# Windowed attention in units of 64 queries of two heads, with 320 keys, in place of 128 queries of one head with 384

## The chip, the cores and the metric

The kernel runs on one core of a Trainium2 chip. The core has five engines with a queue each: TensorE (PE), whose weight loads are shown apart as PEld, VectorE (DVE), ScalarE (ACT), GpSimd (POOL), and SyncE (SP), which issues the transfers. The metric is the time of one execution on the device in microseconds; of the kernel before three runs are known, with 440.9 us as their median.

## The reference, cut to what matters

One encoder layer over 1024 tokens of 1024 numbers: a projection into queries, keys, values and gates of two groups of heads, two kinds of attention, gates, an output projection, and a layer norm. The change is in group B, the windowed attention with shared keys. It has 8 query heads and 2 key heads of 64 numbers; a query sees the keys at most 128 tokens away, and a learned sink logit joins the softmax of each head.

```python
def windowed_gqa_with_sink(q, k, v, sink):          # q: (1, 1024, 8, 64); k, v: (1, 1024, 2, 64)
    ...                                             # blocks of 128 queries, bands of 384 keys
    s = jnp.einsum('bnqkgd,bnjkd->bnkgqj', qb, k_band).astype(jnp.float32) * (D ** -0.5)
    valid = (jnp.abs(k_off - q_off) <= SWA_WINDOW)[None] & (k_abs >= 0) & (k_abs < S)
    s = jnp.where(valid[None, :, None, None], s, MASK_VALUE)
    p = jax.nn.softmax(jnp.concatenate([s, sink_col], axis=-1), axis=-1)[..., :-1]
    out = jnp.einsum('bnkgqj,bnjkd->bnqkgd', p.astype(v.dtype), v_band)
...
    y_b = windowed_gqa_with_sink(qb, kb, v_b, sink)
    mixed = jnp.concatenate([y_a * jax.nn.silu(z_a), y_b * jax.nn.silu(z_b)], axis=-1)
    y = jnp.einsum('bse,ed->bsd', mixed, w_out[layer])
    x = layer_norm(DEEPNORM_ALPHA * x + y, ln_gain[layer], ln_bias[layer])
```

## The kernel before, in words

**The work.** The projection of x is made of 128x512 matmuls in f16 (L430), with weights and x split into a high and a low f16 part, so that three passes give one f32 product. What it delivers is turned to queries and keys, which are split into high and low parts again (high by ACT at L298 or L300, low by DVE at L304 or by POOL at L306), and group B's get their rotary positions on the way (L364 to L368). The weights of a projection are scaled and split on the way in as well: ACT makes the high part (L240), POOL scales and makes the low part (L245, L246).

**Units.** Attention runs in 128 units, first 64 of group B and then 64 of group A. A unit (g, p, j, t) of group B is the block t of 128 queries of head j of head pair p; the order is p, then j, then t. Four units in a row are a quad. What is done for a unit i and for its quad q, by stage:

- `stage_qk`: two matmuls (L860, L861: the query tile holds high and low parts on its 128 partitions, and is multiplied by the keys' high and then low parts) put scores for up to three blocks of 128 keys, 384 columns, in a bank of PSUM; a unit at either end of the sequence has two blocks, 256 columns. DVE adds the mask `bm`, changes the sign, writes the scores to `sn` in SBUF and keeps the row's minimum, the sink included, as `nm` (L870, called "the reduction" below; the profile shows its accumulator read as a row of its own).
- `stage_exp`: ACT writes the exponentials into the same bank (L885), one column more than the scores for the sink; the row sums are kept in `sm`.
- `stage_tr`, one step later: ACT copies the exponentials as high f16 parts (L895), DVE subtracts to get the low parts (L896), and a DMA transposes both (L899).
- `stage_pv`, once for a quad: PE multiplies the transposed probabilities by the values (L925), four units side by side in one bank: 128 partitions of queries, 4 x 64 columns.
- `stage_on`, once for a quad, a step after: DVE takes the reciprocals of the four sums (L934) and multiplies the 128x256 bank by them (L937) into the tile `on`, whose partitions are 128 tokens, and whose free axes are block, head of the pair, and 64 numbers.
- `stage_ot`, for the quads of the second head: PE transposes `on` (L948), and DVE multiplies it by the gate (L951).

**What sets the order.** A planner writes the program step by step, one unit to a step; a step of group B is planned as 1.88 us. At step i it issues `stage_qk` and `stage_exp` of unit i, `stage_tr` of unit i-1, and every fourth step the stages of a quad. Between them PE gets a share of the projection's matmuls (`pump_to`), so that these fill every pause of attention. Casts, splits and weights wait in queues by engine, and are issued when the planned use of an engine (`book`, whose costs the planner adds up) leaves room, or when a unit needs them (`need`). Scores have four banks: the matmul of unit i+4 has to wait for the subtraction L896 of unit i. Each engine works its instructions off in the order written; semaphores hold an instruction until what it reads is there.

Of the kernel before, what the change touches and what calls it, by code (L numbers as in the profile page):

```python
# [7 lines left out]
F32 = mybir.dt.float32  # L8
F32R = mybir.dt.float32r
F16 = mybir.dt.float16  # L10
# [55 lines left out]
def hybrid_block(ctx, tc, xT, x, wt, wv, wo, bias, sink, gain, lbias, cos, sin, bmask, out):  # L66
# [68 lines left out]
    bm = const.tile([128, 384], F32, name="bm")  # L135
    sk = const.tile([128, 8], F32, name="sk")
    nsk = const.tile([128, 8], F32, name="nsk")


    raws, parts, tiles = {}, {}, {}  # L140

    def stk(kind):
        if kind == "q":
            return tiles["kq"].tile([128, S], F16, tag="qs", name="qs", bufs=4)
# [143 lines left out]
    stks = {}  # L288

    def own(kind, p, j):  # L290
        if (kind, p, j) not in stks:
            stks[kind, p, j] = stk(kind)
        return stks[kind, p, j]

    def split_hl(h, l, src, scaled, eng):
# [21 lines left out]

    def split_q(p, half, src, dep=None):
        col = dep is None
        ops, high = [], []  # L320
        prio = 0 if dep is None else 1
        eng = "pool" if dep and clock["step"] is not None else "dve"
        for j in range(2):
            a, o = slice(64 * j, 64 * j + 64), slice(64 - 64 * j, 128 - 64 * j)
            hi, lo = split_hl(lambda j=j, a=a: place(own("q", p, j), a, half, col),
                              lambda j=j, o=o: place(own("q", p, j), o, half, col),
                              taken_from(src, a, col), dep is None, eng)
# [491 lines left out]
    st = {}  # L819
    on = {}  # L820

    def geom(u):
# [16 lines left out]
    def stage_qk(u):  # L839
        g, p, j, t = u  # L840
        n, _m = geom(u)
        ps = bank("s")
        lo = max(t - 1, 0) * 128
        if g == "a":
            q = stks["q", p, j][:, 128 * t:128 * t + 128]
            sl = [stks[w, p, j][:, lo:lo + n] for w in ("kh", "kl")]
            b = (t > 0) + (t == 7)
            bias_t, op = st["bias", p, j]
            need(op)
            bias_t = bias_t[:, BWIN[b]:BWIN[b + 1]]  # L850
            init = 3e38
        else:
            q = stks["q", f"b{p}", j][:, 128 * t:128 * t + 128]
            kv = p // 2
            sl = [stks[w, "b", kv][:, lo:lo + n] for w in ("kh", "kl")]
            bias_t = bm[:, 128 if t == 0 else 0:(128 if t == 0 else 0) + n]
            h = 2 * p + j
            init = nsk[:, h:h + 1]
        book("dve", 0.25 + 0.0011 * n + (0.08 if g == "b" and t < 2 else 0))
        nc.tensor.matmul(ps[:, :n], q, sl[0], start=True, stop=False)  # L860
        nc.tensor.matmul(ps[:, :n], q, sl[1], start=False, stop=True)  # L861
        s0 = sns[units.index(u) % 2]
        sn = s0 if g == "a" else s0[:, 384 - n:]
        if g == "b" and t < 2:
            nc.vector.tensor_copy(s0[:, 384:385], nsk[:, h:h + 1])
        elif g == "a" and p == 0 and j == 0 and t < 2:
            nc.vector.memset(s0[:, 368:384], -NEG)
        nm = ap.tile([128, 1], F32, tag="nm", name="nm", bufs=6)
        c = min(p, 1) if g == "b" else 2
        nc.vector.tensor_tensor_reduce(sn[:, :n], ps[:, :n], bias_t, sg[:, c:c + 1], init,  # L870
                                       op0=ALU.add, op1=ALU.min, accum_out=nm)
        st[u, "sn"] = sn
        st[u, "ps"] = ps
        st[u, "nm"] = nm
# [31 lines left out]
    def stage_pv(q):  # L906
        ps = st[q, "o"] = bank("t")
        for m in range(4):
            u = units[4 * q + m]
            g, p, j, t = u  # L910
            tr = st.pop((u, "tr"))
            mms = []
            n, c = geom(u)
            w = VE if g == "a" else HD
            for i in range(c):
                k = max(t - 1, 0) + i
                d = slice(0, min(128, n - 128 * i))
                if g == "a":
                    v = [va[p][d, k, VE * (2 * j + e):VE * (2 * j + e) + (VE, HD)[e]] for e in range(2)]
                else:  # L920
                    v = [vb[d, k, p // 2, e, :] for e in range(2)]
                ph, pl = tr[d, 2 * i, :], tr[d, 2 * i + 1, :]
                mms += [(ph, v[0], w), (ph, v[1], HD), (pl, v[0], w)]
            for i, (a, b_, e) in enumerate(mms):
                nc.tensor.matmul(ps[:, w * m:w * m + e], a, b_, start=(i == 0), stop=(i == len(mms) - 1))  # L925

    def stage_on(q):
        g, p, j, h = quad(q)
        ps = st.pop((q, "o"))
        ri = ap.tile([128, 4], F32, tag="ri", name="ri", bufs=4)  # L930
        book("dve", 0.55)
        w = VE if g == "a" else HD
        o = ps[:, :4 * w].rearrange("p (m e) -> p m e", e=w)
        nc.vector.reciprocal(ri, o[:, :, HD] if g == "a" else st.pop((q, "sm")))  # L934
        if j == 0:
            on[g, p, h] = ap.tile([128, 4, 2, HD], F32, tag="on", name="on", bufs=2)
        nc.vector.tensor_mul(on[g, p, h][:, :, j, :], o[:, :, :HD], ri.unsqueeze(2).to_broadcast([128, 4, HD]))  # L937

    def stage_ot(q):
        g, p, j, h = quad(q)  # L940
        if j == 0:
            return
        need(*stk_ops.get(f"zb{p}" if g == "b" else f"z{p}", ()))
# [200 lines left out]
    def m_kq(i, keys):  # L1144
        for key in keys:
# [1 line left out]
            z = zt[ZP[i][n // 2]][:, (ZL, ZH)[n % 2]]  # L1147

            def home(key=key):
                tag = "ks" if i == 2 else "qs"  # L1150
                t = tiles["kq"].tile([128, 2, 512], F16, tag=tag, name=f"{key}_{i}", bufs=8 if i == 2 else 4)
                part[key, i] = t[:, 0], t[:, 1]

            m_split((key, i), z, prio=1.7, home=home)
# [228 lines left out]
    for i in range(-LD, NU + LO):  # L1383
# [96 lines left out]
def _host(inputs):  # L1480
# [36 lines left out]
    arr["sink"] = np.ascontiguousarray(np.broadcast_to(np.asarray(inputs["sink_logits"]), (128, 8)))  # L1517
# [9 lines left out]
    d = np.arange(384)[None, :] - 128 - np.arange(128)[:, None]  # L1527
    arr["bmask"] = np.where(np.abs(d) <= 128, 0.0, NEG).astype(np.float32)
    return arr

# [20 lines left out]
```

## Time and profile before

| | |
|---|---|
| median of three runs (lowest, highest) | 440.9 us (440.69, 441.12) |
| the profiled execution | 441.08 us, span 439.3 us |
| PE busy in the span | 434.3 us, 99% |
| DVE busy | 334.9 us, 76% |
| ACT busy | 314.1 us, 72% |
| POOL busy | 280.4 us, 64% |
| DMA share over the span | q1 75.1% of 16 engines |
| granted TensorE clock | 1.00 |

The 64 units of group B are worked from about 120 us of the span to about 238 us, those of group A after that, beside what is left of the projection and then the output projection with the norm. In a row of the timeline stand the start, the duration, the engine, the line and operation, what is written and read, the shape, and in square brackets how long the engine sat idle before it and for whom. A row that ends in "x2" holds two instructions. The waits of an engine are summed in rows "engine, line, waited for: us, times, longest". [...]

### The profile page before, as it was taken

What the parts mean: (1) busy time and instruction counts of PE and PEld (TensorE: products, weight loads), DVE (VectorE), ACT (ScalarE), POOL (GpSimd) and SP (SyncE); (2) the same over time, 40 slices, a digit from 0 to 9 for tenths busy, and PEclk for the clock granted to TensorE, in tenths of its full rate; (3) what the DMA queues carried; (4) which work ended last, traced back from release to release, by engine and by line L of the source; (5) the groups of instructions that cost most, each with busy time, mean ns of one, the idle gap of its engine ahead of it and who ended that gap; (6) DMA issues with size and microseconds to landing.
All of it is one profiled execution on the core that took longest, in us unless ns stands there. A gap on an engine that the chain in (4) does not pass through costs nothing.

```text
span 439.3 us, 9382 instructions
## 1 busy us (share of the span) xinstructions
PE 434.3 (99%) x3225; PEld 253.6 (58%) x3225; DVE 334.9 (76%) x819; ACT 314.1 (72%) x661; POOL 280.4 (64%) x300
## 2 busy tenths in 40 slices
PE   9999999999999999999999999999999999999996
PEld 9997754444445555565555565655656555444444
DVE  5978976775978798888788987878788855675455
ACT  5839789768688888888988969888888773332321
POOL 0110074578438648779998789897989881058585
PEclk9999999999999999999999999999999999999999
DMA  8921469994428999996959999989899969711113
GB/s 272 406 84 60 128 233 327 283 279 168 120 55 196 198 180 176 202 175 124 180 123 213 209 195 219 212 185 181 155 192 227 161 122 354 316 48 73 72 73 120
DMA packets 128815, 80.12 MB, mean 182 GB/s; under 512 B 97280, under 2 KB 106496, under 8 KB 128768
## 3 DMA queue, kind: packets, MB, share of 16 engines
q1 hardware_dynamic: 128624, 79.33, 75.1%
q8 instruction: 25, 0.41, 0.4%
q14 instruction: 22, 0.18, 0.1%
q10 hardware_dynamic: 144, 0.20, 0.1%
HBM read 48.01 MB, written 8.42 MB: 128 GB/s over the span
## 4 chain that ended last, share of the span: by engine, by line
PE 94%; POOL 3%; ACT 1%; DVE 0%; issue 0%; POOLq 0%; ACTq 0%
PE ps_pj L430 50%; PE ps_s L1178 8%; PE ps_t L925 7%; PE ps_s L537 6%; PE ps_s L860 4%; PE ps_s L861 4%; PE ps_pj L1178 4%; PE ps_pj L537 3%; PE ps_t L537 3%; PE ps_t L1178 2%; PE ps_t L948 2%; POOL xr L1287 2%; POOL xr L1288 2%; PE ps_t L463 1%; ACT xr L1285 1%; POOL xr L1238 0%
## 5 line engine op out<-in xcount | busy, mean ns | idle before, releaser
L430 PE MATMUL ps_pj<-xf,wh 128*128 128x512 f16 x672 | 201.3, 379 | 0.0
L430 PE MATMUL ps_pj<-xf,wl 128*128 128x512 f16 x336 | 127.3, 379 | 0.0
L430 PEld LDWEIGHTS <-wh 128*128 128x128 f16 x672 | 63.7, 98 | 59.8
L885 ACT ACTIVATE ps_s<-sn,nm 128x385 f32<-128x385 f32 (+3 forms) x128 | 70.9, 554 | 30.0 <-DVE nm L870 29.5
L896 DVE SCALAR_TENSOR_TENSOR split<-ps_s,split 128x384 f16<-128x384 f32 (+1 forms) x128 | 66.8, 522 | 18.1 <-ACT split L895 16.7
L245 POOL TENSOR_SCALAR wr<-wr,wsc 128x512 f32<-128x512 f32 x32 | 23.0, 718 | 66.5 <-ACT wh L240 62.3
L895 ACT ACTIVATE split<-ps_s 128x384 f16<-128x384 f32 (+1 forms) x128 | 58.2, 455 | 1.6
L430 PEld LDWEIGHTS <-wl 128*128 128x128 f16 x336 | 32.8, 98 | 38.1
L870 DVE CUSTOM_DVE_ANT_0 sn<-ps_s,bias,sg 128x368 f32<-128x368 f32 (+1 forms) x64 | 36.2, 566 | 13.7 <-PE ps_s L861 13.1
L870 DVE CUSTOM_DVE_ANT_0 sn<-ps_s,bm,nsk 128x384 f32<-128x384 f32 (+1 forms) x64 | 40.8, 638 | 6.1 <-PE ps_s L861 5.6
L246 POOL TENSOR_TENSOR wl<-wr,wh 128x512 f16<-128x512 f32 x32 | 39.9, 1247 | 2.7
L861 PE MATMUL ps_s<-ks,qs 128*128 128x384 f16 (+2 forms) x128 | 39.7, 310 | 0.0
L860 PE MATMUL ps_s<-ks,qs 128*128 128x384 f16 (+2 forms) x128 | 39.7, 310 | 0.0
L925 PEld LDWEIGHTS <-tr 128*128 128x128 f16 (+1 forms) x1056 | 36.2, 98 | 2.4
L1178 PEld LDWEIGHTS <-A 128*128 128x128 f16 x216 | 20.1, 98 | 20.7
L347 POOL COPY ks<-ks 64x512 f16<-64x512 f16 x40 | 26.2, 656 | 4.7 <-ACT ks L298 2.1
L1285 ACT ACTIVATE xr<-xr,nmr,rstd 128x1024 f32<-128x1024 f32 x6 | 7.4, 1240 | 27.0 <-POOL nmr L1232 27.0
L1213 DVE SCALAR_TENSOR_TENSOR xr<-ps_s,yc,xr 128x512 f32<-128x512 f32 (+1 forms) x22 | 15.8, 724 | 13.9 <-PE ps_s L1178 13.5
L1178 PEld LDWEIGHTS <-m 128*128 128x128 f16 x144 | 13.9, 98 | 15.9 <-issue 0.2
L537 PEld LDWEIGHTS <-xf 128*128 128x128 f16 x192 | 18.6, 98 | 7.3
L240 ACT ACTIVATE wh<-wr,wsc 128x512 f16<-128x512 f32 x32 | 22.7, 710 | 0.0
L1287 POOL TENSOR_TENSOR xr<-xr,gb 128x512 f32<-128x512 f32 x13 | 16.9, 1303 | 8.1 <-ACT xr L1285 8.1
(217 smaller groups left out, 899.0 us busy)
## 6 DMA issues: line engine op xcount, KB each, us to landing
wr<-in_wt SPq DMA_DIRECT2D x32, 256.0 KB, 3.2
ws<-in_wt SPq DMA_DIRECT2D x15, 512.0 KB, 6.6
wor<-in_wo SPq DMA_DIRECT2D x20, 256.0 KB, 3.8
xr<-in_x SPq DMA_DIRECT2D x8, 512.0 KB, 10.5
wob<-in_wo SPq DMA_DIRECT2D x14, 256.0 KB, 3.8
out<-xr SPq DMA_DIRECT2D x14, 256.0 KB, 2.0
bias<-in_bias SPq DMA_DIRECT2D x8, 440.0 KB, 4.3
wvraw<-in_wv SPq DMA_DIRECT2D x9, 320.0 KB, 5.6
```

The costliest lines, as they stand in the source:

```text
L246: nc.gpsimd.tensor_sub(l, raw, h)
L347: nc.gpsimd.tensor_copy(place(t, o, half, col), place(t, a, half, col))
L430: nc.tensor.matmul(ps, a[:, k % 4, :], mv, start=(k == 0 and i == 0), stop=(k == KT - 1 and i == 2))
L537: nc.tensor.matmul(ps[:, :320], lh[:, ts], rh[:, cs], start=(k == ko[0] and i == 0), stop=(k == ko[-1] and i == 2))
L860: nc.tensor.matmul(ps[:, :n], q, sl[0], start=True, stop=False)
L861: nc.tensor.matmul(ps[:, :n], q, sl[1], start=False, stop=True)
L870: nc.vector.tensor_tensor_reduce(sn[:, :n], ps[:, :n], bias_t, sg[:, c:c + 1], init, op0=ALU.add, op1=ALU.min, accum_out=nm)
L885: nc.scalar.activation(pt[:, :m], sn[:, :m], AF.Exp, bias=nm, scale=-1.0, accum_out=acc)
L895: nc.scalar.activation(hl[:, :m, 0, :], src, AF.Copy, scale=PSCALE)
L896: nc.vector.scalar_tensor_tensor(hl[:, :m, 1, :], src, PSCALE, hl[:, :m, 0, :], op0=ALU.mult, op1=ALU.subtract)
L925: nc.tensor.matmul(ps[:, w * m:w * m + e], a, b_, start=(i == 0), stop=(i == len(mms) - 1))
L1178: nc.tensor.matmul(ps[:, cs], lh[:, 128 * t:128 * t + 128], rh[:, cs], start=(fresh and e == 0 and n == 0), stop=(e == len(terms) - 1 and ...
```

## The change

A unit of group B is now 64 queries of both heads of a pair: partitions 0 to 63 hold the 64 queries of the first head, 64 to 127 the same queries of the second. With b from 0 to 15 as the block of 64 queries, the band of keys is 320 wide in place of 384; it is 256 wide for b = 1 and 14, and 192 for b = 0 and 15. The number of units is the same (16 blocks x 4 pairs in place of 8 blocks x 8 heads). The tuple keeps its form: j is now the half of the sequence, and t the block in it.

What follows from it in the code: the query tiles of a pair lie interleaved in one tile of twice the length (two of them in place of four); the mask is 128x320 and the sink values are by pair. Exponentials, split, transposes and the multiplication by the values still go over whole blocks of 128 keys, three or two, so parts of `sn` that no score fills are set by a memset at some units. A column of sink has to be copied at 8 units, where it was 16. The bank of a quad now has, on 128 partitions, 64 tokens of two heads, and four such blocks side by side; `on` wants 128 tokens on the partitions and the heads along the free axis. So the multiplication by the reciprocals goes in four pieces of 64 partitions x 128 columns; two of the four read one half of the partitions and write the other. The transposes L948 with their gate now follow quads 1 and 3 of each pair instead of 2 and 3. At the first unit of a half both heads' queries must be ready for that half.

```diff
     def geom(u):
         g, p, j, t = u
+        if g == "b":
+            b, lo, edge = b_span(u)
+            return 64 * min(b + 3, 16) - lo, 2 if edge else 3
...
-            q = stks["q", f"b{p}", j][:, 128 * t:128 * t + 128]
+            b, lo, edge = b_span(u)
+            q = own("q", f"b{p}", 0)[:, 128 * b:128 * b + 128]
...
-            bias_t = bm[:, 128 if t == 0 else 0:(128 if t == 0 else 0) + n]
-            h = 2 * p + j
-            init = nsk[:, h:h + 1]
+            c0 = lo - 64 * (b - 2)
+            bias_t = bm[:, c0:c0 + n]
+            init = nsk[:, p:p + 1]
...
-        sn = s0 if g == "a" else s0[:, 384 - n:]
-        if g == "b" and t < 2:
-            nc.vector.tensor_copy(s0[:, 384:385], nsk[:, h:h + 1])
+        sn, at0 = s0, 0
+        if g == "b":
+            sn, at0 = s0[:, 128:] if edge else s0, 0 if b == 1 else lo % 128
+            if b < 2:
+                nc.vector.tensor_copy(s0[:, 384:385], nsk[:, p:p + 1])
+            for at_, pad in ((0, 320), (3 if p == 0 else None, 0), (15, 128)):
+                if b == at_:
+                    nc.vector.memset(s0[:, pad:pad + 64], -NEG)
...
-        nc.vector.tensor_tensor_reduce(sn[:, :n], ps[:, :n], bias_t, sg[:, c:c + 1], init,
+        nc.vector.tensor_tensor_reduce(sn[:, at0:at0 + n], ps[:, :n], bias_t, sg[:, c:c + 1], init,
...
-        book("dve", 0.55)
+        book("dve", 0.55 if g == "a" else 1.1)
...
+        if g == "b":
+            j, h = h, j
         if j == 0:
             on[g, p, h] = ap.tile([128, 4, 2, HD], F32, tag="on", name="on", bufs=2)
-        nc.vector.tensor_mul(on[g, p, h][:, :, j, :], o[:, :, :HD], ri.unsqueeze(2).to_broadcast([128, 4, HD]))
+        if g == "a":
+            nc.vector.tensor_mul(on[g, p, h][:, :, j, :], o[:, :, :HD], ri.unsqueeze(2).to_broadcast([128, 4, HD]))
+            return
+        for e in range(2):
+            r = slice(64 * e, 64 * e + 64)
+            for m in range(2):
+                nc.vector.tensor_mul(on[g, p, h][64 * m:64 * m + 64, 2 * j:2 * j + 2, e, :], o[r, m::2, :],
+                                     ri[r, m::2].unsqueeze(2).to_broadcast([64, 2, HD]))
...
-            if u[0] == "b" and u[3] in (0, 4):
-                need(*stk_ops[f"b{u[1]}", u[2], u[3] // 4])
+            if u[0] == "b" and u[3] == 0:
+                need(*[o for j in range(2) for o in stk_ops[f"b{u[1]}", j, u[2]]])
```

Two places in the order of DVE show it. The first is around units 34 and 35, in the third head pair, where the quad of units 24 to 27 is divided by its sums; `sn0` and `sn1` are the two buffers of the scores' negatives, `nm` the minima, `split3` a buffer of the exponentials' high and low parts. Before:

```order
L870 ISA sn0_1138,nm_2500<-ps_s_2497,bm_124,nsk_126,sg_117 128x384
L304 SCALAR_TENSOR_TENSOR ks_2379<-ps_pj_2361,ks_2359 64x64x8
L304 SCALAR_TENSOR_TENSOR ks_2381<-ps_pj_2361,ks_2364 64x64x8
L896 SCALAR_TENSOR_TENSOR split3_1135<-ps_s_2442,split3_1135 128x3x128
L934 RECIPROCAL ri_2509<-sm_2170 128x4
L937 TENSOR_TENSOR on_2258<-ps_t_2448,ri_2509 128x4x64
L870 ISA sn1_1139,nm_2526<-ps_s_2523,bm_124,nsk_126,sg_117 128x384
```

The same place after, with lines 897, 310, 923, 961 and 972 for 870, 304, 896, 934 and 937:

```order
L897 ISA sn0_1138,nm_2525<-ps_s_2522,bm_124,nsk_126,sg_117 128x320
L310 SCALAR_TENSOR_TENSOR ks_2391<-ps_pj_2373,ks_2371 64x64x8
L310 SCALAR_TENSOR_TENSOR ks_2393<-ps_pj_2373,ks_2376 64x64x8
L923 SCALAR_TENSOR_TENSOR split3_1135<-ps_s_2458,split3_1135 128x2x128
L961 RECIPROCAL ri_2534<-sm_2181 128x4
L972 TENSOR_TENSOR on_2536<-ps_t_2470,ri_2534 64x2x64 x4
L897 ISA sn1_1139,nm_2555<-ps_s_2552,bm_124,nsk_126,sg_117 128x320
```

The order is the same; the reductions on either side are narrower, and four multiplications stand where one stood, ahead of the reduction of unit 35.

The second place, also on DVE, is the border between the second pair and the third, at units 31 to 33. Before, the first blocks of a head have two blocks of keys, and so has the last:

```order
L870 ISA sn1_1139,nm_2404<-ps_s_2401,bm_124,nsk_126,sg_117 128x256
L896 SCALAR_TENSOR_TENSOR split0_1132<-ps_s_2374,split0_1132 128x3x128
L865 COPY sn0_1138<-nsk_126 128x1
L870 ISA sn0_1138,nm_2425<-ps_s_2421,bm_124,nsk_126,sg_117 128x256
L896 SCALAR_TENSOR_TENSOR split1_1133<-ps_s_2401,split1_1133 128x2x128
L865 COPY sn1_1139<-nsk_126 128x1
L870 ISA sn1_1139,nm_2446<-ps_s_2442,bm_124,nsk_126,sg_117 128x384
```

After, with the multiplication by the gate (L989, L951 before) of the second pair's tokens behind it:

```order
L892 MEMSET sn1_1139 128x64
L897 ISA sn1_1139,nm_2419<-ps_s_2415,bm_124,nsk_126,sg_117 128x192
L923 SCALAR_TENSOR_TENSOR split0_1132<-ps_s_2386,split0_1132 128x2x128
L889 COPY sn0_1138<-nsk_126 128x1
L892 MEMSET sn0_1138 128x64
L897 ISA sn0_1138,nm_2441<-ps_s_2436,bm_124,nsk_126,sg_117 128x192
L923 SCALAR_TENSOR_TENSOR split1_1133<-ps_s_2415,split1_1133 128x2x128
L889 COPY sn1_1139<-nsk_126 128x1
L897 ISA sn1_1139,nm_2462<-ps_s_2458,bm_124,nsk_126,sg_117 128x256
L989 SCALAR_TENSOR_TENSOR z5_1287<-ps_t_2464,zc_101,z5_1287 128x512
```

Two memsets are new here, the reductions are narrower, and the gate's multiplication of the fifth tile stands four units earlier than before.

More of the change, by code (lines that the diff above doesn't have):

```diff
@@ L290, in own @@
     def own(kind, p, j):
+        if kind == "q":
+            if (kind, p) not in stks:
+                stks[kind, p] = q_tile("qs")
+            t = stks[kind, p]
+            return t[:, S * j:S * j + S] if p in range(4) else t
         if (kind, p, j) not in stks:
-            stks[kind, p, j] = stk(kind)
+            stks[kind, p, j] = stk()
         return stks[kind, p, j]
@@ L319, in split_q, with at_q @@
         col = dep is None
+        def at_q(j, a):
+            t = own("q", p, j)
+            if col:
+                return place(t, a, half, True)
+            return t[a].rearrange("p (b h c) -> p b h c", h=2, c=64)[:, 8 * half:8 * half + 8, j, :]
         ops, high = [], []
@@ L324, in split_q @@
             a, o = slice(64 * j, 64 * j + 64), slice(64 - 64 * j, 128 - 64 * j)
-            hi, lo = split_hl(lambda j=j, a=a: place(own("q", p, j), a, half, col),
-                              lambda j=j, o=o: place(own("q", p, j), o, half, col),
-                              taken_from(src, a, col), dep is None, eng)
+            hi, lo = split_hl(lambda j=j, a=a: at_q(j, a), lambda j=j, o=o: at_q(j, o),
+                              taken_from(src, a, True) if col else src[a].rearrange("p (b c) -> p b c", c=64),
+                              dep is None, eng)
             high.append((enq("act", hi, dep, prio=prio, after=28 if dep else 0), lo))
```

38 lines of the change are left out of this document (24 added, 14 removed).

## Prediction

> **What bounds the kernel now.** I read the page's busy shares and its chain of work first, then the stretch from 120 to 238 us in which group B's units run, and what DVE and ACT wait for in it.
>
> ```profile
> PE 434.3 (99%) x3225; PEld 253.6 (58%) x3225; DVE 334.9 (76%) x819; ACT 314.1 (72%) x661; POOL 280.4 (64%) x300
> PE 94%; POOL 3%; ACT 1%; DVE 0%; issue 0%; POOLq 0%; ACTq 0%
> 120.00:238.00 118.00, 118.00 (x1001) 66.48 (x1000) 97.13 (x277) 101.47 (x258) 88.86 (x87) 1.00 0.86 163
> ACT ps_s L885 <- DVE nm L870: 12.6, 19, 1.3
> DVE split L896 <- ACT split L895: 10.0, 22, 1.3
> DVE sn L870 <- PE ps_s L861: 5.6, 12, 1.2
> DVE z L395 <- ACT z L394: 1.4, 2, 1.2
> DVE wom L970 <- DMA wor<-in_wo: 1.3, 2, 0.8
> DVE ks L304 <- ACT ks L298: 0.4, 1, 0.4
> DVE split L896 <- POOL wl L246: 0.2, 1, 0.2
> ```
>
> The third row gives the stretch, its length and the busy time of PE, PEld, DVE, ACT and POOL: PE is busy for all 118.0 us at clock 1.00, so PE's own work sets the time, and a column less is time saved as long as PE never starves. DVE is busy for 97.1 us and waits 18.9 us by the rows below; the 2.0 us left are short gaps. Only 5.6 us of the waits are for PE. The 10.0 us for ACT are no free room: ACT waits for DVE's minima for 12.6 us in the same stretch. The two engines hand a unit to and fro, so that DVE's path is longer than its busy time.
>
> **PE's saving.** The scores of one unit with 384 columns and of one with 256:
>
> ```profile
> 185.64 0.33 PE L860 MATMUL ps_s<-ks,qs 128*128 128x384 f16 x1
> 185.81 0.33 PE L861 MATMUL ps_s<-ks,qs 128*128 128x384 f16 x1
> 185.97 0.59 PE L430 MATMUL ps_pj<-xf,wh 128*128 128x512 f16 x2
> ...
> 176.79 0.27 PE L860 MATMUL ps_s<-ks,qs 128*128 128x256 f16 x1
> 176.90 0.27 PE L861 MATMUL ps_s<-ks,qs 128*128 128x256 f16 x1
> 177.01 0.59 PE L430 MATMUL ps_pj<-xf,wh 128*128 128x512 f16 x2
> ```
>
> From start to start a matmul takes 0.165 us at 384 columns and 0.110 at 256, so 0.43 ns a column. Before, 48 units of 384 and 16 of 256 make 22,528 columns; after, 48 of 320, 8 of 256 and 8 of 192 make 18,944. The 3,584 columns less, in two matmuls each, are worth 7,168 x 0.43 ns = 3.1 us. Nothing else changes on PE but the place of the transposes L948.
>
> **DVE's saving and its new work.** The groups by shape, then a piece of DVE's timeline around one division by the sums, and an old memset:
>
> ```profile
> L870 DVE CUSTOM_DVE_ANT_0 sn<-ps_s,bm,nsk 128x384 f32<-128x384 f32 x48 | 32.3, 672 | 6.0 <-PE ps_s L861 5.6
> L870 DVE CUSTOM_DVE_ANT_0 sn<-ps_s,bm,nsk 128x256 f32<-128x256 f32 x16 | 8.6, 535 | 0.1
> L937 DVE TENSOR_TENSOR on<-ps_t,ri 128x256 f32<-128x256 f32 x32 | 13.6, 424 | 1.1
> L865 DVE COPY sn<-nsk 128x1 f32<-128x1 f32 x16 | 2.3, 144 | 0.0
> ...
> 176.30 1.41 DVE L304 SCALAR_TENSOR_TENSOR ks<-ps_pj,ks 64x512 f16<-64x512 f32 x2
> 177.74 0.56 DVE L896 SCALAR_TENSOR_TENSOR split<-ps_s,split 128x384 f16<-128x384 f32 x1
> 178.21 0.17 DVE L934 RECIPROCAL ri<-sm 128x4 f32<-128x4 f32 x1
> 178.42 0.42 DVE L937 TENSOR_TENSOR on<-ps_t,ri 128x256 f32<-128x256 f32 x1
> 178.76 0.53 DVE L870 CUSTOM_DVE_ANT_0 sn<-ps_s,bm,nsk 128x256 f32<-128x256 f32 x1
> ...
> 240.83 0.07 DVE L867 MEMSET sn<- 128x16 f32 x1
> ```
>
> The reduction L870 costs 672 - 535 = 137 ns for 128 columns, 1.07 ns a column: 3,584 columns less are -3.8 us over group B.
>
> The multiplication L937 becomes four of 64 partitions x 128 columns. One takes 424 - 137 = 0.29 us, since time goes by columns, not partitions. How fast they follow one another, no row of this operation shows; two bounds do. The subtraction at 177.74 ends at 178.30 and the reciprocal has started at 178.21; the multiplication ends at 178.84 and the next reduction has started at 178.76. With such an overlap of 0.08 us a piece costs 0.21, four cost 0.84, and against today's 0.34 (178.42 to 178.76) a quad costs 0.50 more. The other bound is the pair L304 in the first timeline row: two subtractions on different halves of the partitions, 1.41 us together with 0.69 for one alone, end at 177.71, and the full-width subtraction behind them starts at 177.74. There nothing overlaps: 0.03 us lie between an end and the next start. So held, a piece costs 0.31, four 1.24, and a quad 0.90 more. I take 0.90, since the nearest row in kind, 64 partitions after 64 others, is the pair: reading or writing moves to the other half between any two pieces, and again to the reduction behind the last. [...]
>
> 14 of the 16 quads of group B are divided inside the stretch: 14 x 0.90 = +12.6 us. Nine new memsets, wider than the one in the row but of its kind, add 9 x 0.07 = +0.6 (zero to 1 us); eight copies less, 0.144 each less the overlap of 0.08, are -0.5. Together DVE gets 12.6 - 3.8 + 0.6 - 0.5 = +8.9 us in the stretch.
>
> **Who waits for that.** Behind the four pieces stands the reduction of the next unit, and ACT's exponential waits for its minimum; ACT's copy comes after the exponential, and DVE's own subtraction after the copy. That the waits for ACT don't take up the new work is seen behind a division in the trace:
>
> ```profile
> 186.18 0.42 DVE L937 TENSOR_TENSOR on<-ps_t,ri 128x256 f32<-128x256 f32 x1
> 186.52 0.67 DVE L870 CUSTOM_DVE_ANT_0 sn<-ps_s,bm,nsk 128x384 f32<-128x384 f32 x1
> 187.11 0.55 DVE L896 SCALAR_TENSOR_TENSOR split<-ps_s,split 128x384 f16<-128x384 f32 x1
> ...
> 187.23 0.59 ACT L885 ACTIVATE ps_s<-sn,nm 128x385 f32<-128x385 f32 x1 [1.10 <-DVE nm L870]
> 187.84 0.71 ACT L240 ACTIVATE wh<-wr,wsc 128x512 f16<-128x512 f32 x1
> ...
> 188.96 0.56 DVE L896 SCALAR_TENSOR_TENSOR split<-ps_s,split 128x384 f16<-128x384 f32 x1 [0.70 <-ACT split L895]
> ```
>
> The subtraction next after the division (187.11) has no wait that could shrink. The one after (188.96) waits 0.70 us for ACT, which itself sat 1.10 us for the minimum that came after the division. A later division makes ACT later and leaves that wait. So I keep the 10.0 us in DVE's path. Of the other 3.3 us (1.4, 1.3, 0.4, 0.2) I keep half, 1.7; the bounds are none and all.
>
> **The sum.** DVE's path in the stretch: 97.1 + 2.0 + 10.0 + 1.7 = 110.8 us, and +8.9 makes 119.7. PE needs 118.0 - 3.1 = 114.9. DVE is over by 4.8. Two corrections: waits for PE ahead of the first division can't be used, and some lateness may stand at the end without PE stopping.
>
> ```profile
> DVE sn L870 <- PE ps_s L861: 1.1, 4, 0.5
> ...
> 185.50 0.56 DVE L896 SCALAR_TENSOR_TENSOR split<-ps_s,split 128x384 f16<-128x384 f32 x1
> ...
> 187.26 0.33 PE L860 MATMUL ps_s<-ks,qs 128*128 128x384 f16 x1
> ...
> L870 DVE CUSTOM_DVE_ANT_0 sn<-ps_s,bias,sg 128x368 f32<-128x368 f32 x48 | 28.6, 596 | 12.8 <-PE ps_s L861 12.7
> ```
>
> The first row is of 120 to 139 us, ahead of the first division: +1.1. The subtraction of 185.50 ends at 186.06 and frees the bank that the scores at 187.26 take, a slack of 1.2 us, about the smallest in group B: -1.2. PE's stall is 4.8 + 1.1 - 1.2 = 4.7 us, where before it had none. Against PE's saving that is +1.6. Two divisions fall behind 238 us, 1.8 us more work over some seven units; there the reduction of group A waits 12.7 us for PE in 64 units, 0.2 a unit, 1.4 in seven, so +0.4. In all +2.0 us on 441.08 (439.3 of span and 1.8 around it) is 443.1; the profiled execution lies 0.2 above the median, so 442.9 us. With all of the other 3.3 us kept it is 444.5, and with only half of the reduction's saving coming through as well, 446; with none of them kept, 441.2.
>
> Where PE would stop first can be named. At unit 40 the second half of the third pair begins, and now needs both heads' queries, where the second head's were needed at unit 44:
>
> ```profile
> 188.71 0.69 POOL L245 TENSOR_SCALAR wr<-wr,wsc 128x512 f32<-128x512 f32 x1 [0.20 <-PE ps_t L925]
> 191.28 1.15 POOL L306 TENSOR_TENSOR qs<-rp_raw,qs 64x512 f16<-64x512 f32 x1
> ...
> 193.42 0.27 PE L860 MATMUL ps_s<-ks,qs 128*128 128x256 f16 x1
> ```
>
> POOL makes the last low part until 192.43; unit 40 starts at 193.42, and with 40/64 of PE's saving would start at 191.5. POOL's work there stands behind the scaling at 188.71, whose weights' high part ACT makes at 187.84, behind the exponential that waits for the minimum. If DVE is as late as before, PE stops some 0.9 us. I don't add it, since the same lateness is in the 4.7; without a late DVE the minimum comes 1.6 us earlier, and it vanishes. Interleaved queries cost ACT and POOL nothing: the same 64x512 elements, in runs of 64.
>
> **Rivals.** One, on the other side: the pieces overlap as full-width neighbours do, 0.50 a quad. DVE then gets 7.0 - 3.8 + 0.6 - 0.5 = +3.3, its path is 114.1 against 114.9, with the corrections 114.0, and PE never stops: 440.9 - 3.1 = 437.8, with all other waits kept 438.5; I say 438.2. It decides from a piece of 0.26 us down, 0.70 a quad: there the stall is 1.9 us, and with the 0.4 the time is 0.8 us under before. For it speak the overlaps of 0.08; against it, the pair L304. [...]
>
> Two: the waits for ACT shrink when DVE becomes the late engine. Each microsecond of the 10.0 that goes is one less of stall: with 2.0 gone the time is as before, with 4.7 gone it is 438.2. ACT's 16.5 us without work in the stretch speak for it, its 12.6 us of waits for DVE against it.
>
> Three: the two effects cancel within 0.2%, 0.9 us, which is about what a measurement can tell from no change: partly shrinking waits, or none of the 3.3 us kept, 441.2.
>
> **How the numbers follow.** Slower by the forecast 0.60 (its own range 441.8 to 446.0), overlap 0.16, shrinking waits 0.12, cancelled 0.12. Faster is 0.28, same 0.12, slower 0.60. The range from 438.0 to 446.0 takes in the rivals' middle and leaves out the ends.
>
> **What would show it.** Right: each piece lasts 0.28 to 0.30 us and the next starts after its end; L860 at 320 columns takes 0.137 us from start to start; PE's busy time in group B falls by 3 us while idle PE appears, first near unit 40, with DVE's subtraction named as what it waits for; DVE's waits for PE all but vanish, and those for ACT stay near 10. Wrong: pieces starting 0.21 us apart, or DVE's waits for ACT falling by 3 us and more.

## The result, and the profile after

The changed kernel takes 450.3 us (449.84 to 451.4) where the kernel before took 440.9 beside it: slower by 2.17%, with a 95% interval of 2.01 to 2.32%. The forecast was slower too, but 442.9 us with a range up to 446.0, so 2.0 us of loss where there are 9.4.

The page's busy shares and the chain of work of the changed kernel, whose profiled span is 448.4 us where it was 439.3:

```profile
PE 434.6 (97%) x3225; PEld 252.7 (56%) x3225; DVE 341.2 (76%) x867; ACT 313.9 (70%) x663; POOL 281.1 (63%) x300
PE 68%; ACT 13%; DVE 7%; issue 7%; POOL 4%; DMA 1%; POOLq 0%; DVEq 0%; ACTq 0%
```

PE's share of the chain falls from 94% to 68%: the chain now runs through ACT and DVE for a fifth of the span. To see where the time went, take the same piece of work in both traces: from the reduction of unit 0 to that of unit 84, 20 units into group A, where DVE is about to be waiting for PE regularly again. First the stretch of the kernel before (its bounds, its length, then the busy time of PE, PEld, DVE, ACT and POOL):

```profile
123.56:276.42 152.86, 152.86 (x1321) 86.63 (x1320) 127.82 (x363) 132.83 (x325) 121.67 (x124) 1.00 0.94 177
```

The main waits of ACT and DVE in it, of the kernel before:

```profile
ACT ps_s L885 <- DVE nm L870: 16.9, 25, 1.3
DVE split L896 <- ACT split L895: 12.4, 25, 1.3
DVE sn L870 <- PE ps_s L861: 7.8, 15, 1.4
DVE z L395 <- ACT z L394: 1.4, 2, 1.2
DVE ks L304 <- ACT ks L298: 0.4, 1, 0.4
```

The same stretch of the changed kernel:

```profile
123.44:285.42 161.98, 153.25 (x1320) 85.97 (x1319) 135.69 (x410) 132.60 (x327) 121.57 (x124) 1.00 0.86 166
```

Its main waits of ACT, DVE and PE, which now appears (line 912 is the exponential, 923 the subtraction, 922 ACT's copy, 897 the reduction, 883 the scores, 972 the division, 986 the transposes):

```profile
ACT ps_s L912 <- DVE nm L897: 27.5, 24, 2.2
DVE split L923 <- ACT split L922: 19.0, 34, 1.2
PE ps_s L882 <- DVE split L923: 3.1, 7, 1.2
PE ps_t L986 <- DVE on L972: 2.7, 4, 0.7
DVE ks L310 <- ACT ks L304: 1.3, 2, 0.7
PE ps_s L882 <- POOL qs L312: 1.2, 1, 1.2
DVE qs L310 <- ACT qs L304: 1.1, 2, 0.6
DVE sn L897 <- PE ps_s L883: 0.9, 3, 0.3
DVE z L408 <- ACT z L407: 0.3, 1, 0.3
```

DVE's time in the stretch adds up as work, waits for ACT (all rows in which DVE waits for it, the copy L895 or L922 and a few others), waits for PE, other waits, and short gaps (the length less the rest). Busy is the time in which some instruction runs, so it is shorter where the same instructions overlap more. The same sum for the kernels of the experiments stands below in one table; all figures are from such rows.

| us | length | DVE busy | waits for ACT | waits for PE | other waits | gaps |
|---|---|---|---|---|---|---|
| before | 152.9 | 127.8 | 14.2 | 7.8 | 1.5 | 1.5 |
| after | 162.0 | 135.7 | 21.7 | 0.9 | 0.5 | 3.2 |
| one piece | 150.8 | 122.7 | 17.2 | 6.4 | 2.5 | 2.0 |
| before in four pieces | 162.7 | 140.1 | 17.9 | 1.9 | 0.2 | 2.7 |
| four that don't cross | 155.5 | 129.1 | 21.0 | 3.3 | 0.5 | 1.7 |
| spread | 159.4 | 136.5 | 15.1 | 3.2 | 0.5 | 4.1 |
| casts first | 159.1 | 135.3 | 19.2 | 0.9 | 0.5 | 3.1 |
| division ahead | 157.1 | 134.1 | 17.5 | 0.7 | 1.9 | 2.9 |
| ahead, casts first | 155.2 | 133.7 | 15.1 | 1.2 | 2.5 | 2.7 |
| masked | 159.7 | 126.9 | 10.9 | 17.6 | 3.0 | 1.4 |

From before to after the stretch is 9.1 us longer, all of the loss: DVE's work and gaps +9.5, its waits for PE used up (-6.9), other waits -1.0, and its waits for ACT +7.5. The forecast had the first two about right and the last at nothing.

The pieces themselves are as forecast. The group of the new reductions and that of the pieces, in the changed kernel:

```profile
L897 DVE CUSTOM_DVE_ANT_0 sn<-ps_s,bm,nsk 128x320 f32<-128x320 f32 x48 | 29.0, 604 | 0.8 <-PE ps_s L883 0.5
L972 DVE TENSOR_TENSOR on<-ps_t,ri 64x128 f32<-64x128 f32 x64 | 18.5, 289 | 1.2
```

DVE's timeline around one division, up to the subtraction that waits after it:

```profile
189.24 0.17 DVE L961 RECIPROCAL ri<-sm 128x4 f32<-128x4 f32 x1
189.44 1.20 DVE L972 TENSOR_TENSOR on<-ps_t,ri 64x128 f32<-64x128 f32 x4
190.67 0.61 DVE L897 CUSTOM_DVE_ANT_0 sn<-ps_s,bm,nsk 128x320 f32<-128x320 f32 x1
...
193.06 0.56 DVE L923 SCALAR_TENSOR_TENSOR split<-ps_s,split 128x384 f16<-128x384 f32 x1 [0.77 <-ACT split L922]
```

ACT's timeline between them:

```profile
191.33 0.59 ACT L912 ACTIVATE ps_s<-sn,nm 128x385 f32<-128x385 f32 x1 [1.91 <-DVE nm L897]
191.85 0.19 ACT L912 ACTIVATION_READ_ACCUMULATOR ps_s<-sn,nm 128x1 f32 x1
191.94 0.71 ACT L241 ACTIVATE wh<-wr,wsc 128x512 f16<-128x512 f32 x1
192.56 0.47 ACT L922 ACTIVATE split<-ps_s 128x384 f16<-128x384 f32 x1
```

PE now stands idle for 8.7 us of the stretch (161.98 less 153.25), where it had no idle time: 3.1 us of that for the subtraction, 3.4 for the division itself (2.7 in the row above, 0.7 in another), 1.2 for POOL, and 0.8 for a transfer; the rest are short gaps.

Four pieces last 1.20 us and the reduction starts 1.23 us after the first of them, 0.31 a piece. Then one sees the loss grow: ACT stands 1.91 us for the minimum; the cast of weights L241, which has nothing to do with this unit, is written behind the exponential and starts only after it; ACT's copy L922 stands behind the cast; and DVE waits 0.77 us for the copy.

### The profile page after: what moved, and what is told of

Same layout as the page of the kernel before. It is cut to its first block, busy times and chain, and to the rows that moved or that the text cites. A ratio compares the mean times of both kernels' runs of the same rounds, so it can differ in the third digit from the quotient of the medians.

```text
span 448.4 us, 9426 instructions
## 1 busy us (share of the span) xinstructions
PE 434.6 (97%) x3225; PEld 252.7 (56%) x3225; DVE 341.2 (76%) x867; ACT 313.9 (70%) x663; POOL 281.1 (63%) x300
## 4 chain that ended last, share of the span: by engine, by line
PE 68%; ACT 13%; DVE 7%; issue 7%; POOL 4%; DMA 1%; POOLq 0%; DVEq 0%; ACTq 0%
PE ps_pj L443 31%; PE ps_s L1220 8%; PE ps_s L550 6%; PE ps_t L952 4%; ACT ps_s L912 4%; PE ps_pj L1220 3%; PE ps_pj L550 3%; PE ps_t L550 3%; ACT split L922 3%; DVE on L972 3%; PE ps_t L1220 2%; PE ps_s L882 2%; PE ps_s L883 2%; DVE split L923 2%; POOL xr L1329 1%
## 5 line engine op out<-in xcount | busy, mean ns | idle before, releaser
L922 ACT ACTIVATE split<-ps_s 128x384 f16<-128x384 f32 (+1 forms) x128 | 58.2, 455 | 1.6
L882 PE MATMUL ps_s<-ks,qs 128*128 128x320 f16 (+3 forms) x128 | 38.1, 298 | 4.5 <-DVE split L923 3.1
L883 PE MATMUL ps_s<-ks,qs 128*128 128x320 f16 (+3 forms) x128 | 38.1, 298 | 0.0
L897 DVE CUSTOM_DVE_ANT_0 sn<-ps_s,bm,nsk 128x320 f32<-128x320 f32 (+2 forms) x64 | 36.8, 575 | 1.0 <-PE ps_s L883 0.5
L1220 PEld LDWEIGHTS <-m 128*128 128x128 f16 x198 | 19.0, 98 | 20.9 <-issue 0.2
L1220 PEld LDWEIGHTS <-A 128*128 128x128 f16 x162 | 15.1, 98 | 15.8 <-DVE A L1154 0.4
L883 PEld LDWEIGHTS <-qs 128*128 128x128 f16 x128 | 12.5, 98 | 19.8 <-issue 6.4
L241 ACT ACTIVATE wh<-wr,wsc 128x512 f16<-128x512 f32 x32 | 22.7, 710 | 0.0
```

Source lines behind the costliest of these rows:

```text
L897: nc.vector.tensor_tensor_reduce(sn[:, at0:at0 + n], ps[:, :n], bias_t, sg[:, c:c + 1], init, op0=ALU.add, op1=ALU.min, accum_out=nm)
L922: nc.scalar.activation(hl[:, :m, 0, :], src, AF.Copy, scale=PSCALE)
L1220: nc.tensor.matmul(ps[:, cs], lh[:, 128 * t:128 * t + 128], rh[:, cs], start=(fresh and e == 0 and n == 0), stop=(e == len(terms) - 1 and ...
```

## The experiments

**One piece.** Is it the division at all?

```diff
-        for e in range(2):
-            r = slice(64 * e, 64 * e + 64)
-            for m in range(2):
-                nc.vector.tensor_mul(on[g, p, h][64 * m:64 * m + 64, 2 * j:2 * j + 2, e, :], o[r, m::2, :], ...)
+        nc.vector.tensor_mul(on[g, p, h][:, 2 * j:2 * j + 2, :, :].rearrange("p b e d -> p (b e) d"), o,
+                             ri.unsqueeze(2).to_broadcast([128, 4, HD]))
```

> The changed kernel, but the multiplication by the reciprocals is one instruction again, 128x256, and puts the products in the places in which they lie in the bank, so that tokens and heads are mixed in what follows; everything else, the planner's cost of 1.1 included, stays. My theory (the four pieces are the whole loss): TensorE saves its 3.1 us and waits for nothing, 437.8 to 439 us. Rival (the other parts cost too: the transposes after quads 1 and 3, both heads needed at unit 40, the edges in a row): the waits at those places stay, and the time is above 441 us.

438.8 us, a ratio of 0.9949 to before (0.9931 to 0.9966). The main waits of DVE, ACT and PE in this kernel's stretch from unit 0 to unit 84:

```profile
DVE split L923 <- ACT split L922: 16.4, 29, 1.2
ACT ps_s L912 <- DVE nm L897: 14.1, 21, 1.3
DVE sn L897 <- PE ps_s L883: 6.4, 11, 1.1
PE ps_t L952 <- DMA tr<-split: 0.6, 1, 0.6
```

So the pieces are the whole loss, 11.5 us of it: everything else of the change makes the kernel faster by 2.1 us, some 1 us less than PE's 3.1. The rows also show what became of the cheaper reductions. DVE works 5.2 us less than before in the stretch and waits 3.0 us more for ACT: it comes to the subtraction earlier, and ACT's copy isn't there as much earlier.

**Before in four pieces.** The division alone, put into the kernel before.

```diff
-        nc.vector.tensor_mul(on[g, p, h][:, :, j, :], o[:, :, :HD], ri.unsqueeze(2).to_broadcast([128, 4, HD]))
+        for m in range(2):
+            for e in range(2):
+                r = slice(64 * e, 64 * e + 64)
+                nc.vector.tensor_mul(on[g, p, h][r, m::2, j, :], o[r, m::2, :],
+                                     ri[r, m::2].unsqueeze(2).to_broadcast([64, 2, HD]))
```

(For group A the line stays.)

> The kernel before, but group B's multiplication by the reciprocals is done in four pieces of 64 partitions x 128 columns, ordered so that each starts on the other half of the partitions than the one ahead of it; results are the same. Nothing else of the change is in it. By my sum (0.90 us more a quad, the waits for ScalarE stay at 10 us): path of VectorE 110.8 + 12.6 + 1.1 - 1.2 = 123.3 us against TensorE's 118.0, so +5.3 and +0.4 in group A, 446.6 us. Rival (each late minimum makes ScalarE late, and its pile of work makes VectorE wait again): the waits for ScalarE grow to 16 us or more, and the time is 452 us or more.

451.2 us, 1.0233 (1.0217 to 1.0248): 10.2 us slower, where the sum of the prediction gives 5.7. Two of its waits in the stretch:

```profile
ACT ps_s L885 <- DVE nm L870: 28.1, 27, 2.0
DVE split L896 <- ACT split L895: 14.6, 26, 1.3
```

ACT's waits for the minima go from 16.9 to 28.1 us, and DVE's for ACT from 14.2 to 17.9 in all: +3.7. That is less than the rival of the expectation had, so in this kernel the waits explain 3.7 of the 4.5 us that the sum missed. With the +3.0 of the one-piece kernel they make 6.7 of the 7.5 us by which the changed kernel's waits for ACT grew: both halves of the change make DVE wait for ACT, one by coming early to the copy, the other by making ACT late. And since this kernel, with none of the savings, is only 0.9 us slower than the changed one, the 3.1 us of PE and the 3.8 us of reductions, with the rest of the change, bring nearly nothing once the pieces are there.

**Four pieces that don't cross.** The number of instructions or their crossing?

```diff
-        for e in range(2):
-            ...
+        for k in range(4):
+            nc.vector.tensor_mul(on[g, p, h][:, 2 * j:2 * j + 2, k % 2, :], o[:, k // 2::2, :],
+                                 ri[:, k // 2::2].unsqueeze(2).to_broadcast([128, 2, HD]))
```

> The changed kernel, but each of the four pieces is over all 128 partitions x 128 columns and stays in the partitions it reads, so no piece starts on another half (tokens and heads are mixed in what follows). Four instructions of the same length are left, and what goes is only that they can't overlap. If they then start 0.21 us apart, a quad costs 0.50 more than one piece in place of 0.90. My sum gives 438 us. Rival (the loss grows with the lump even below the point where my sum sees VectorE over): half of the way from the one-piece kernel to the changed one, 443 to 446 us.

443.0 us, 1.0037 (1.0019 to 1.0054), at the lower end of the rival's range. DVE's timeline around one division of this kernel:

```profile
186.22 0.88 DVE L970 TENSOR_TENSOR on<-ps_t,ri 128x128 f32<-128x128 f32 x4
187.03 0.60 DVE L897 CUSTOM_DVE_ANT_0 sn<-ps_s,bm,nsk 128x320 f32<-128x320 f32 x1
```

Four pieces now take 0.81 us from start to the next start, 0.20 each, and not 1.23. That no piece overlaps its neighbour where it starts on another half of the partitions is thus shown, and costs 0.42 us a quad, 6.7 us of DVE's time in 16 quads; the kernel without it is 7.3 us faster. (These pieces also cover 128 partitions in place of 64. That 64 alone don't forbid an overlap is seen in the changed kernel, where the multiplication L381 over 128 partitions starts at 94.98 us and lasts 0.98, and the subtraction L312 over the first 64 starts at 95.88, 0.08 us before its end.) The step below, from one piece to four that overlap, is 0.47 us a quad, 7.5 us of DVE's time, and costs 4.2 us. The prediction's sum gives 438 here, where it sees DVE just under PE: the loss begins earlier than the sum says, as waits for ACT are at 21.0 us already. From there to the changed kernel they grow by 0.7 us only: the crossing costs its own work and little more, while the waits come with the smaller lump already.

**Spread over two units.** The sum of the work, or the lump ahead of one minimum?

```diff
+        if m == 2 and q in on_late:
+            on_late.pop(q)()          # pieces three and four, behind the next subtraction
```

> The changed kernel, with two of the four pieces a unit later: pieces one and two stand where all four stood, three and four behind the next subtraction. The work of VectorE is the same to the instruction. Theory A (it is the sum of VectorE's work that counts): no change, 449.5 to 451 us. Theory B (it is the lump of 1.2 us ahead of one minimum, for which ScalarE waits about 2 us a time and whose own pile then delays VectorE): ScalarE's waits for the minima fall from 21 us to 16 or less, and the time by 3 us or more, 447 us or less.

448.6 us, 1.0173 (1.0154 to 1.0193), 1.8 us faster than the changed kernel: neither answer. In the table the waits for ACT fall by 6.6 us with about the same work, and ACT's for the minima from 27.5 to 22.3, as theory B has it. But one of PE's waits, 2.7 us in the changed kernel, is much longer here:

```profile
PE ps_t L992 <- DVE on L976: 7.4, 6, 2.9
```

The last pieces now come too late for the transposes (L992), so that PE stands 4.7 us longer there; by that row this is what takes back most of the gain, but no run tests it alone.

**Casts first.** ACT's order alone, at the unit behind each division.

```diff
-        if i < NU:
+        late = m == 2 and 0 <= q and i < 64
+        if i < NU and not late:
             stage_exp(units[i])
...
         pop("act", NA if 0 in held or i < 105 and len(held) < 5 else 2)
+        if late:
+            stage_exp(units[i])
```

> The changed kernel with its work unchanged; only ScalarE's order differs: at the unit behind each division by the sums, the cast or split that stood behind the exponential now stands ahead of it, at some thirteen places. Theory B (the lump: ScalarE stands for the late minimum with ready work behind it, and that work then delays its copy, for which VectorE waits): ScalarE does 0.6 us of work in each of these waits, VectorE's waits for ScalarE fall by 4 us or more of 21.7 between the reductions of units 0 and 84, and the time falls by 2 to 5 us, to 445 to 448 us. Theory A (VectorE's sum of work): its work is the same, so no change, 449.5 to 451 us.

447.4 us, 1.0141 (1.0123 to 1.0159): 3.0 us faster, with not an instruction less. DVE's waits for ACT fall by 2.5 us, not the 4 expected, and ACT's for the minima by 4.0. The two rows of this kernel's stretch:

```profile
ACT ps_s L912 <- DVE nm L897: 23.5, 23, 2.2
DVE split L923 <- ACT split L922: 16.6, 32, 1.2
```

This shows the mechanism of the timeline above: ready work of ACT stood behind the late exponential.

**Division ahead of the subtraction.** DVE's order alone.

```diff
+        if m == 1 and 0 <= q < 16:
+            stage_on(q)
         if 0 <= i - LT < NU:
             stage_tr(units[i - LT])
...
-        if m == 1 and 0 <= q < NU // 4:
+        if m == 1 and 0 <= q < NU // 4 and q >= 16:
             stage_on(q)
```

> The changed kernel with its work unchanged; only VectorE's order differs: each division of group B stands ahead of the subtraction that it stood behind, so between the reduction of one unit and the subtraction of the unit before. Theory B (VectorE's path holds waits for ScalarE's copy that work placed ahead of them can fill): the subtraction that waits for ScalarE now does so behind 1.4 us of work and finds its copy ready, VectorE's waits for ScalarE fall by some 0.3 us a quad or more, and the time by 3 us or more, 447 us or less. Theory A (VectorE's sum of work): no change, 449.5 to 451 us. The next reduction is no earlier than before by the order, so ScalarE's waits for the minima need not fall.

444.8 us, 1.0087 (1.0068 to 1.0106): 5.5 us faster than the changed kernel. Three of the waits of its stretch:

```profile
ACT ps_s L912 <- DVE nm L897: 22.6, 24, 2.0
DVE split L923 <- ACT split L922: 14.8, 26, 1.2
PE ps_s L882 <- DVE split L923: 5.3, 7, 1.9
```

The waits for ACT's copy are 4.2 us less, a little under the 0.3 us a quad expected: the division now runs while ACT makes its copy. DVE is busy for 1.6 us less with the same instructions. PE waits for the subtraction alone, for 5.3 us in place of 3.1; its waits for the division are gone.

**Both orders.**

> The changed kernel with the division ahead of the subtraction and the casts ahead of the exponential, both orders at once. If they take away different waits, the gains add: 3.0 us from the casts, which were measured, and 3 us or more from the division's place, 444.5 us or less. If both take away the same waits, 446 to 447.5 us, about that of the casts alone. Neither theory has it below the one-piece kernel's 438.8 us.

444.3 us, 1.0076 (1.0055 to 1.0098), 6.1 us faster than the changed kernel. The 444.5 us of the first expectation are met, but not by its reason: the division's place alone had brought 5.5 us, the casts add 0.6 and not 3.0, and the intervals of the two kernels overlap. DVE's waits for ACT are 15.1 us in the stretch, 6.6 less than in the changed kernel and about what they were before (14.2). These do add (2.5 and 4.2 us less apart), and the stretch is 1.9 us shorter than with the division's place alone; why the whole kernel gains only 0.6 by it isn't shown. Against the kernel before, what is left of the loss, 3.2 us, goes with DVE's own work, which is 5.9 us more than before.

**Two versions that cross no partitions.** They were made to keep the narrower scores without the pieces. In the first, two units share a tile of transposed probabilities, and the multiplication by the values puts the tokens in rows itself; the sums of the rows are moved by small transfers.

```diff
+                    nc.sync.dma_start(sm2[64 * m_:64 * m_ + 64, e::2], sm[e::2, m_::2])    # four a quad
...
+                    t2 = st[(4 * q + m) // 2, "tr2"]
+                    ph, pl = (t2[d, 2 * i + k_].rearrange("p m c -> p (m c)")[:, m % 2::2] for k_ in range(2))
```

> A version that keeps 64 queries of two heads and 320 keys, but needs no crossing of partitions: the two heads of a token lie side by side (query partitions are token times two plus head), two units share one tile of transposed probabilities, and the multiplication by the values takes every second column of the pair as its stationary operand, so its result has 128 tokens on the partitions for each head. The division is one 128x256 instruction again, with the planner's cost of 0.55. The 128x4 sums go to that order by four small transfers a quad; these cost no engine time. If the pieces are the whole loss, the time is that of the one-piece kernel, 438 to 439.5 us, and faster than before by 0.3 to 0.7%. Rival: the strided stationary operand makes the weight loads (98 ns now) longer, or the transfers (2 us and more to land) come late for the reciprocals, or they delay SyncE's queue: 441 us or more.

484.5 us, 1.0992 (1.097 to 1.1014). SyncE's queue shows why (start, duration of the issue, what is moved):

```profile
149.56 1.22 SPq L929 DMA_TRANSPOSE tr<-split  x1
150.84 2.57 SPq L935 DMA_DIRECT2D sm<-sm  x4
153.52 1.23 SPq L929 DMA_TRANSPOSE tr<-split  x1
154.80 0.77 SPq L1010 DMA_DIRECT2D wor<-in_wo  x1
```

Issuing a transfer of half a kilobyte takes SP 0.64 us, about as long as one of 256 KB (0.77 in the last row, mostly 0.53 to 0.59); four of them come on top of four transposes of 1.2 us and the loads. Once issued, nothing is much slower: a load of `wor` lands after 3.7 us in the median and a transpose after 3.7 (3.7 and 3.5 in the changed kernel). So what SP loads and transposes is issued late, as this kernel's waits between 120 and 246 us show:

```profile
DVE wom L1018 <- DMA wor<-in_wo: 21.8, 5, 5.7
PE ps_t L965 <- DMA tr<-split: 10.3, 10, 3.6
```

"These cost no engine time" was the mistake: SP's queue is an engine's time as well, here 2.57 us of it for the four of a quad. The granted clock is lower too, 0.986 over the profiled execution, with 0.7 to 0.8 in four of the page's forty slices; how much of the loss that makes isn't shown. The strided stationary operand is not the cause; in the groups by line a weight load takes 98 ns, as before:

```profile
L965 PEld LDWEIGHTS <-tr 128*128 128x128 f16 x912 | 35.1, 98 | 23.7 <-issue 12.4 <-DMA tr<-split 9.2
```

In the second, DVE multiplies once by masked reciprocals and PE adds up the halves, with both orders from above:

```diff
+            nc.vector.tensor_mul(on[q], o.unsqueeze(2).to_broadcast([128, 4, 2, HD]),
+                                 ri.unsqueeze(3).to_broadcast([128, 4, 2, HD]))
...
+                nc.tensor.matmul(ps[:, 64 * i:64 * i + 64], o[:, i].rearrange("p h e -> p (h e)"), id2, start=True, stop=True)
```

> A version that keeps 64 queries of two heads and 320 keys, with the orders of the two runs before (division ahead of the subtraction, casts ahead of the exponential), and with no crossing of partitions on VectorE: a quad's bank is multiplied once, 128x512, by the reciprocals times a 0/1 mask by head, which leaves zeros in the places of the other head; TensorE then multiplies this by two identities of 64 set on top of each other, which adds up the halves and so gives 128 rows of two heads by 64 tokens, for one quad at a time; the gate's multiplication is 128x256 for each quad. The reciprocals are taken earlier, a step after the quad's last exponential, and GpSimd multiplies them by the mask. VectorE's division takes some 0.6 us in place of 1.24, plus 0.2 for the reciprocals as now, and the gate 0.05 a quad more, so 0.3 us a quad above one piece. At the rate between the one-piece kernel and the division ahead (6.0 us for 14.4 us of VectorE's work) that is 2 us: 440 to 441.5 us, about the kernel before. If what matters is the lump ahead of a minimum and little else, 439 us, faster than before by 0.4%. If the matmuls against the identities are slower than the transposes (109 ns at 128 columns), 442 us or more.

447.95 us, 1.0165 (1.0142 to 1.0188), which is the third answer of the expectation. DVE isn't late any more, as the waits of its stretch show:

```profile
DVE sn L903 <- PE ps_s L889: 17.1, 21, 1.8
DVE split L929 <- ACT split L928: 9.8, 19, 1.2
```

But PE has got the work. Its timeline at one quad:

```profile
165.73 1.00 PE L994 MATMUL ps_t<-id,on 128*128 128x64 f32 x8
166.56 1.04 PE L964 MATMUL ps_t<-vb,tr 128*128 128x64 f16 x30
```

A quad has four such matmuls, which the trace shows as eight; the next work starts 0.83 us after the first, where two transposes of 128 columns took 2 x 0.11 (the four L986 of the changed kernel start at 198.44 us, and the work behind them 0.44 later). That is 0.61 us a quad, 9.8 us in all, and PE is busy for all 159.71 us of the stretch. Each of the eight has a weight load of its own, and takes about as long at 64 columns (0.10 us) as a transpose at 128 (0.11): their number seems to count here, and not the columns, which no run tests alone. Without it the version would lie near 438; no kernel shows that.

## Why the prediction was wrong

- **PE's saving, 3.1 us: right.** A score matmul of 320 columns takes 0.14 us from start to start (below), and the one-piece kernel is 2.1 us faster; of the 1.0 us that is missing, 0.6 is a wait for transposes. The sign named for it, 3 us less of PE's busy time, came only there (150.2 us in the stretch, where it was 152.9); in the changed kernel PE is busy for 153.3. A matmul in front of a stop is shown with its whole length, 0.38 us, where otherwise 0.22 pass to the next start; the rows of PE's waits count 14 stops in the stretch, which makes an estimated 2.2 us.
- **A piece, 0.29 us, and 0.31 from start to start: right**, and so the choice between the two bounds (0.20 and 0.31 in the runs), and that the time goes by columns (0.28 for a piece over 128 partitions, 0.29 over 64). From the first start to the reduction behind them, four pieces that cross take 1.23 us, four that don't 0.81.
- **DVE's new work, +8.9 us and 1.8 in group A: slightly too much**; the stretch shows 7.9 of work and 1.7 of gaps. That interleaved queries cost ACT and POOL nothing was right: a high part of them takes ACT 0.61 us and a low part takes POOL 1.15, in both kernels.
- **Where PE would stop first: wrong.** It does stop at unit 40, for POOL's last low part as named, 1.20 us where 0.9 were named. But before that it stops at units 30, 31 and 33 already (0.42, 0.18 and 1.17 us), where the narrow units at the ends of the sequence follow one another, each time for the subtraction; and then 0.72 us for the division. Of PE's timeline in the changed kernel, the longest of these, the scores of unit 39, and unit 40:

```profile
180.93 0.27 PE L882 MATMUL ps_s<-ks,qs 128*128 128x256 f16 x1 [1.17 <-DVE split L923]
...
193.66 0.30 PE L882 MATMUL ps_s<-ks,qs 128*128 128x320 f16 x1
193.80 0.30 PE L883 MATMUL ps_s<-ks,qs 128*128 128x320 f16 x1
...
196.59 0.31 PE L882 MATMUL ps_s<-ks,qs 128*128 128x320 f16 x1 [1.20 <-POOL qs L312]
```

- **"So I keep the 10.0 us in DVE's path": this step failed.** In the longer stretch the wait for ACT's copy is 12.4 us before and 19.0 after, and all waits for ACT are 14.2 and 21.7. Two things were left out of it. The 3.8 us that the reductions save were taken off DVE's path in full, though nothing made ACT's copy come as much earlier; 3.0 us of waits came in their place (one piece). (The prediction saw a part of this, 446 us with half of that saving, as the end of its range.) And a later minimum was seen to leave a wait as it is, where it makes it longer: ACT's other work is written behind the exponential, stands with it, and then delays the copy. The rows quoted for it (1.10 us of ACT's wait, the cast L240, 0.70 us of DVE's) showed that chain, and I read only its first half. With 7.5 more the forecast's +2.0 becomes +9.5; less the overestimated work of 1.2 and with the other waits 0.6 higher than taken, +8.9. Of the waits for PE 1.0 more was used up than taken, and the slack of 1.2 doesn't show in this sum: +9.1, as in the stretch.
- **That it is this step and not another**: where orders alone bring the waits back to 15.1 us, the time is 444.3, 1.4 us over the forecast. The same orders also take away PE's waits for the division, so the gain isn't the waits for ACT alone; the spread kernel has 15.1 too, and by its rows loses most of its gain to those waits of PE. Rival two, the waits shrink, was the wrong way round; rival one, the pieces overlap, was refuted by the rows and would not have been faster either: with overlapping pieces the kernel takes 443.0.

What stays open: how the 7.5 us divide between early arrivals and late minima in the changed kernel itself. The two kernels with one cause each have 3.0 and 3.7, which need not add; by the kernels in a row, one piece, four that overlap and four that cross, the steps are 3.0, 3.8 and 0.7.

## What to carry to other kernels

When two engines hand a unit to and fro, a saving on one of them can turn into waits where the other's result doesn't come earlier as well (here 3.0 us of waits for 5.2 us of work less), and a delay can bring waits beside itself, since whatever is written behind the waiting instruction is delayed with it (here the cast L241, behind ACT's wait of 1.91 us): don't take such waits as constants in a sum. Before the work is made cheaper, look at its place: the same 1.2 us cost 5.5 us less where it ran while the other engine worked. An output that had to change partitions was paid here in whole instructions that don't overlap (0.31 us each in place of 0.20), so the layout that the next step wants belongs in the plan of the unit.

## What the runs showed of the hardware that I had not expected

- SP took 0.64 us to issue a transfer of 0.5 KB (2.57 for four), about as for 256 KB (mostly 0.53 to 0.59); the version with 64 of them took 484.5 us, though its division was one piece.
- Each f32 matmul of 128x64 with the identities ran as two instructions of 0.10 us, so that adding with them cost some four times as much as the transposes of the same columns (0.83 us to 0.22 a quad).
